# A hybrid decoder step on one core: three adaLN weight loads issued before x, small vectors issued from the ACT queue

## The chip, the cores and the metric

The kernel runs on one core of a Trainium2 chip. The metric is the device time of one execution in microseconds, as the median of several runs; lower is better.

## The reference, cut to what matters

One inference step of a two-layer trunk for a prompt of 256 tokens and eight samples of eight tokens, 2048 features, float32. Each of the four sub-layers (GLA and S5 side by side, a SwiGLU FFN, an mLSTM, a second SwiGLU FFN) is wrapped in the same way:

```python
def modulate(x, c, ada_w, ada_b, norm_g):
    mod = jax.nn.silu(c.astype(jnp.float32)) @ ada_w + ada_b
    shift, scale, gate = jnp.split(mod[:, None, :], 3, axis=-1)
    return rmsnorm(x, norm_g) * (1.0 + scale) + shift, gate

h, gate = modulate(x, c, p["ab_ada_w"][j], p["ab_ada_b"][j], p["ab_norm_g"][j])
z = (h @ p["ab_w_in"][j]).astype(f32)
...
x = x + (gate * out).astype(x.dtype)
```

So the first big product, `h @ ab_w_in`, needs three things first: x and its norm, `c` after silu, and the products of silu(c) with the shift and scale columns of `ab_ada_w` ([2048, 6144]). Outputs are the normed x and all the updated states.

## The kernel before, in words

**Layout.** Activations are kept feature-major, 16 chunks of [128 features, 320 tokens]. Big products stream their weights through TensorE as 128x128 blocks; each block is split by ACT (`hi`) and VectorE (`lo`) into two float32r parts, and three passes (`hi`, `lo` against `xh`, `hi` against `xl`) are summed in PSUM. The adaLN products and the mixing layers run as background tasks between the blocks.

**adaLN steps.** Class `Ada` cuts the four adaLN products into 192 steps. A step (L477) multiplies silu(c) (`cT`) by one tile of weights of 1024 KB, [128, 4, 512]; four steps give 512 columns of `mod`, which `post` (L459) transposes and adds the bias to. `load` (L444) issues the weight loads on SP's queue, one for every free buffer, as far as `limit`. In the startup there are five buffers (two in `ADAM["raw"]`, one in `ex`, two in `ex2`), and a buffer is free again once its step has run. From step 12 (`TEMP`) on the two of `ex2` are given up. Before the load of step 8 (`L6`), `load` issues four loads of `ab_w_in` (`L2`). The startup works in four groups of features: group g needs 8 steps, the shift and the scale of its 512 features, and then `norm_g` (L744) makes its part of the operand.

**Startup, in the order of the program.** SP loads the identity (L312). ACT's queue loads `c_prompt` and `c_sample` (L630, L631). SP loads x in three pieces, 1024, 1024 and 512 KB (L635 to L637), then 13 small vectors (`items`, L619: biases and gains as rows of 128, 2 to 24 KB each) into `rows` (L640 to L645), then the weights of the first five adaLN steps (L652). PE transposes `c`; VectorE halves it, ACT takes its tanh (L659), VectorE makes `cT` (L661, L662). `load_x` (L836) then squares x on ACT with a sum per token (L843), transposes x on TensorE in 16 chunks of three transposes with a VectorE copy each (L844 to L849), transposes `rows` after chunk 7 (`vectors`, L664), and runs one adaLN step after chunk 7 and one after chunk 15 (L852 to L854). A dozen small VectorE instructions and one product then give the norm factors R (L856, L857). The main program (L2345 to L2365) runs the other steps of group 0, its norm, and then the first products; between products it goes on with steps and loads.

**The order of emission.** Each engine and each queue runs its instructions in the order in which the program emits them, and that order is made by an estimate, `Est` (L130). `Est.note` adds an assumed duration for every instruction; a DMA from SP or ACT goes through one assumed generator, 0.45 us each, and one assumed transfer rate of 360 GB/s (L173 to L180). A background task is resumed when, by the estimate, what it waits for is there (`tick`, L383). `spare` (L497) emits an adaLN step only if the estimate says that its weights have landed. So a changed assumption in `Est` can move instructions everywhere in the program, though it costs nothing itself.

`RQ` (L354) chooses the queue of the 13 vectors: 0 is SP, 1 is ACT. ACT's queue belongs to ScalarE: a DMA that waits there holds up the activations behind it.

Of the kernel before, what the change touches and what calls it, by code (L numbers as in the profile page):

```python
"""One step of the conditioned hybrid decoder trunk (GLA + S5, SwiGLU, mLSTM, SwiGLU) on one core.

Activations are kept feature-major: [128 features, 320 tokens] per chunk, tokens 0-255 the prompt,
256 + 8 b + t the samples. Every big product streams its weights through the tensor engine as
stationary 128x128 blocks. A float32 product is carried by three float32r passes: each operand is
split exactly into hi (what float32r keeps) + lo (the rest), and hi.hi + hi.lo + lo.hi is summed in  # L6
PSUM. Mixing layers and the adaLN products run as background tasks between the blocks of the stream.
"""
# [4 lines left out]
F32 = mybir.dt.float32  # L13
# [19 lines left out]
def _consts():  # L33
    """Constants that depend on shapes alone, packed as [128, NC1 + NC2] (float32), and their offsets."""
# [61 lines left out]
class Mem:  # L96
    """Words of a slab of SBUF, handed out first fit."""
# [32 lines left out]
class Est:  # L130
    """What is known beforehand of the instructions' durations (us). Only the order of emission goes by it: a task is
    resumed when what it issued before should be done, so that the engines seldom wait for one another."""

    def __init__(self):
        self.t = dict.fromkeys(("PE", "DVE", "ACT", "POOL", "SP", "DGE", "DMA"), 0.0)
        self.wr, self.rd, self.alias = {}, {}, {}
        self.end = 0.0
# [23 lines left out]
    def note(self, eng, op, a, k):  # L161
# [11 lines left out]
        if op == "dma_start":  # L173
            if eng == "POOL":
                t = self.t[eng] = t + 1.2
            else:
                self.t[eng] = t + 0.06
                t = self.t["DGE"] = max(self.t["DGE"], t) + 0.45
            t = self.t["DMA"] = max(self.t["DMA"], t + 0.65) + 4e-3 * int(np.prod(out.shape)) / 360
# [30 lines left out]
class Eng:  # L210
    """An engine whose instructions are noted in an Est."""
# [14 lines left out]
class Pair:  # L226
    """Up to 256 output columns of one weight matrix; ks: k-chunks in the order they are used."""
# [6 lines left out]
def trunk(tc, a, o, coff, dbg=None, stop=None):  # L234
# [5 lines left out]
    with (  # L240
# [38 lines left out]
        def mps(keep=False):  # L279
            """A bank for results that are read before the task yields; with keep until drop()."""  # L280
# [14 lines left out]
        def kept():  # L295
            """A bank to be kept, as one of two at most."""
            while len(held) > 1:
                yield GO
            return mps(True)
# [4 lines left out]
        # ------------------------------------------------------------------ fixed memory  # L304
# [42 lines left out]
        # ------------------------------------------------------------------ scheduling  # L347
# [6 lines left out]
        NX, TEMP, RQ, VK, SK, L6, L2 = 2, 12, 0, 7, 8, 8, 4  # L354
# [4 lines left out]
        def due(y):  # L359
            """A task yields a number of ticks to wait at least, GO, or what has to be there before it goes on."""  # L360
            t = est.end
            if y is GO:
                return clock[0] + 1, 0.0
            if isinstance(y, int):
                return clock[0] + y, t
            return clock[0] + 1, max(est.ready(x) for x in y)

        def spawn(gen, rank=5):
            """Tasks of a lower rank are looked at first."""
# [19 lines left out]
        def warm():  # L389
            """A product that nobody reads, lest the tensor engine's clock falls."""  # L390
# [3 lines left out]
        def idle(until):  # L394
            """Nothing for the tensor engine in the program before that time."""
# [8 lines left out]
        def go(gen):  # L404
            """A task that the program waits for."""
# [25 lines left out]
        # ------------------------------------------------------------------ adaLN products  # L431
        class Ada:
# [64 lines left out]
            def spare(self):  # L497
                """A step if its weights are there."""
# [12 lines left out]
            def drip(self):  # L511
                """A step every `gap` ticks up to step `last`, as the program sets them."""
# [8 lines left out]
        # ------------------------------------------------------------------ weight stream  # L521
# [3 lines left out]
        def add(*pairs):  # L525
            """Pairs whose units take turns."""
# [24 lines left out]
        def split_to(n):  # L551
            """hi and lo of the first n half units, which are two chunks of k."""
# [46 lines left out]
        # ------------------------------------------------------------------ startup: vectors  # L599
# [18 lines left out]
        # feature vectors as rows of 128, transposed into columns  # L618
# [8 lines left out]
        # c: silu'd, transposed, padded to 32 columns  # L627
# [4 lines left out]
        # x comes in token-major  # L632
        xt_b = M["S"].get(3 * 2048)
        xt = xt_b.v(3, 2048)
        for i in range(2):  # L635
            sp.dma_start(out=xt[:, i, :], in_=a["x_prompt"][0, i * P:(i + 1) * P, :])
        sp.dma_start(out=xt[0:64, 2, :], in_=a["x_sample"].rearrange("b t d -> (b t) d"))  # L637
        pool.memset(rows, 0.0)
# [7 lines left out]
        ada = Ada()  # L646
        ex = [M["G"].get(2048)]
        ex2 = [M["S"].get(2048) for _ in range(NX)]
        keep = list(ada.free)
        ada.free += [b.v(4, 512) for b in ex + ex2]  # L650
        ada.temp = {id(x): x for x in ada.free[3:]}
        ada.load()  # L652
# [30 lines left out]
        # ------------------------------------------------------------------ RMS norm of x and the operand of the next stage  # L683
        def sq_chunk(k, last=False):
            """Adds x chunk k's squares to the sum (the last two go to the tensor engine by themselves)."""
# [13 lines left out]
        def sums(sq):  # L699
            """Column sums of the tiles in sq, token-major ([128, 3], the third column tokens 192-319)."""  # L700
# [9 lines left out]
        def rsqrt_tok(s, n):  # L710
            """(s / n + EPS) ** -0.5"""
# [4 lines left out]
            # a start within 5% by halving the exponent in the bits, then Newton steps  # L716
# [9 lines left out]
        def rsqrt_t(s, n, skip):  # L726
            """The same for the 320 tokens, in PSUM over all partitions."""
# [16 lines left out]
        def norm_g(L, g, R, ht):  # L744
            """Chunks 4 g to 4 g + 3 of XH + XL = rmsnorm(x) * (1 + scale) + shift."""
# [38 lines left out]
        def norm_h(L):  # L784
            """The first half of the next operand; the rest comes between the first products."""
# [9 lines left out]
        def after_norm(pr):  # L795
            """Marks the pair that begins with half an operand."""
# [9 lines left out]
        def resid(L, k, ps, sq):  # L806
            """x chunk k += gate * ps."""
# [13 lines left out]
        def to_out(k):  # L821
            """x chunk k times the last norm's gains, token-major (block 2: tokens 192-319); all but the scale per token."""
# [13 lines left out]
        def load_x():  # L836
            """Feature-major x, and its norm from the token-major one."""
            sm_b, s_b = M["S"].get(8), M["S"].get(2048)
            sm = sm_b.v(3)
            pool.memset(sm_b.v(8), 1.0)  # L840
            for i in range(3):
# [21 lines left out]
        # ------------------------------------------------------------------ S5: per-state constants  # L863
        # partition = (group of the pair, state); a pair holds two groups of 16 channels
# [4 lines left out]
        def s5_setup():  # L869
            bb = S5["bb"] = S5["bb_b"].v(2, 32, 16)  # L870
            # the imaginary parts of a, b and the states are kept negated, so that Re(c h) is a plain sum of products;
            # powers 1 to 4 of a, and for the scan a^4, a^8 and a^16 as (re, re) and (-im, im)
# [39 lines left out]
            def exp(out, x):  # L912
                """exp to float32 accuracy: 2^n by its exponent bits, the rest by a polynomial."""
# [14 lines left out]
            def sine(out, x, quarter):  # L928
                """sin(x + quarter * pi / 2)."""
# [1515 lines left out]
```

## Time and profile before

| what | us |
|---|---|
| median of three runs | 3397.55 |
| lowest and highest run | 3381.38 and 3400.94 |
| span of the profiled execution, first to last instruction | 3383.8 |

The profile gives no time of the profiled execution apart from its span, 3383.8 us, which lies between the lowest and the highest of the timed runs. The chain of waits is read from the last instruction backwards: each piece is what released the next one. The windows give the busy time of each engine in a stretch, the granted TensorE clock (1.00 is 2.4 GHz) and the rate of the 16 DMA engines together. A wait for a DMA in the queue's own waits is time in which the queue issued nothing.

### The profile page before, as it was taken

The page shows a single profiled execution, that of the slowest core. Times are in us where ns is not written, and L with a number is a line of the kernel's source. Part 1 is how long each engine was busy: PE and PEld are TensorE (multiplying, and loading weights), DVE is VectorE, ACT ScalarE, POOL GpSimd, SP SyncE. Part 2 cuts the span into 40 slices and gives each one's busy share as a digit, 9 for nine tenths or more (in the row PEclk, how much of TensorE's full clock was granted, in tenths as well). Part 3 has the DMA queues.
Part 4 walks back from the last instruction along what each step waited for, and adds up shares of the span by engine and source line. Part 5 has one row for each costly group of instructions (what it writes and reads, how often), then busy time and mean ns, then how long its engine had stood idle before and what let it go on. Part 6 is the DMA issues. An engine that isn't in the chain of part 4 may idle for free.

```text
span 3383.8 us, 57931 instructions
## 1 busy us (share of the span) xinstructions
PE 3287.9 (97%) x22802; PEld 3023.7 (89%) x22802; DVE 1870.4 (55%) x3921; ACT 1327.8 (39%) x2509; POOL 336.9 (10%) x508
## 2 busy tenths in 40 slices
PE   7899889999999999999999999999999999999998
PEld 4687778887877799999998899999899999999997
DVE  3768767663344345445465665566645545545546
ACT  2354554343323333433434433344433343343343
POOL 0225511220000000000031000002200000000002
PEclk9999999999999999999999999999999999999999
DMA  9886678779999954444455665556564444444443
GB/s 305 291 264 219 194 259 305 269 240 322 317 318 320 320 171 149 150 152 148 151 170 145 191 194 144 177 187 206 184 207 149 152 150 150 150 150 150 150 150 100
DMA packets 597794, 686.66 MB, mean 203 GB/s; under 512 B 41097, under 2 KB 495057, under 8 KB 596945
## 3 DMA queue, kind: packets, MB, share of 16 engines
q1 hardware_dynamic: 594464, 680.26, 61.7%
q8 instruction: 179, 2.93, 0.3%
q10 hardware_dynamic: 3056, 2.70, 0.2%
q14 instruction: 95, 0.77, 0.1%
HBM read 643.19 MB, written 39.69 MB: 202 GB/s over the span
## 4 chain that ended last, share of the span: by engine, by line
PE 87%; DMA 5%; DVE 4%; ACT 2%; POOL 1%; issue 1%; SPq 0%; ACTq 0%; DVEq 0%; POOLq 0%
PE mm L220 74%; PE misc L220 8%; PE ada L220 5%; DVE S_slab L220 1%; POOL S_slab L220 1%; DVE lo L220 1%; DMA fix_slab<-in_ffn_ada_w_dram 1%; DVE X_slab L220 1%; DVE G_slab L220 1%; DMA R_slab<-in_state_mlstm_C_dram 1%; DMA fix_slab<-in_ab_w_in_dram 0%; DMA fix_slab<-in_ml_ada_w_dram 0%; DMA G_slab<-in_ab_ada_w_dram 0%; DMA fix_slab<-in_ab_ada_w_dram 0%; ACT hi L220 0%
## 5 line engine op out<-in xcount | busy, mean ns | idle before, releaser
L220 DVE TENSOR_TENSOR lo<-fix_slab,hi 128x512 fp32r<-128x512 f32 (+1 forms) x1556 | 1087.1, 704 | 1173.0 <-ACT hi L220 1168.9
L220 ACT CAST hi<-fix_slab 128x512 fp32r<-128x512 f32 (+1 forms) x1556 | 944.3, 612 | 1425.2 <-PE mm L220 1366.6
L220 PE MATMUL mm<-xh,hi 128*128 128x320 f32 x4704 | 1491.6, 317 | 9.7 <-DVE S_slab L220 5.9
L220 PE MATMUL mm<-xl,hi 128*128 128x320 f32 x4704 | 1460.7, 311 | 0.8 <-DVE xl L220 0.6
L220 PE MATMUL mm<-xh,lo 128*128 128x320 f32 x4704 | 1460.1, 310 | 0.9 <-DVE lo L220 0.9
L220 PEld LDWEIGHTS mm<-xh,hi 128*128 128x128 f32 x4704 | 888.4, 189 | 121.8 <-issue 88.0
L220 PEld LDWEIGHTS mm<-xh,lo 128*128 128x128 f32 x4704 | 889.2, 189 | 2.4 <-DVE lo L220 1.8
L220 PEld LDWEIGHTS mm<-xl,hi 128*128 128x128 f32 x4704 | 888.1, 189 | 2.2 <-DVE xl L220 2.2
L220 PE MATMUL mm<-ffh,hi 128*128 128x320 f32 x1408 | 437.8, 311 | 0.0
L220 PE MATMUL mm<-ffh,lo 128*128 128x320 f32 x1408 | 434.3, 308 | 0.0
L220 PE MATMUL mm<-ffl,hi 128*128 128x320 f32 x1408 | 434.3, 308 | 0.0
L220 POOL TENSOR_TENSOR X_slab<-X_slab 128x320 f32<-128x320 f32 (+1 forms) x117 | 109.9, 940 | 2062.4 <-DVE X_slab L220 2016.1
L220 PEld LDWEIGHTS mm<-ffh,hi 128*128 128x128 f32 x1408 | 264.4, 188 | 18.4 <-issue 17.6
L220 PEld LDWEIGHTS mm<-ffh,lo 128*128 128x128 f32 x1408 | 264.5, 188 | 0.0
L220 PEld LDWEIGHTS mm<-ffl,hi 128*128 128x128 f32 x1408 | 264.3, 188 | 0.0
L220 PE MATMUL ada<-fix_slab 128*32 128x512 f32 x1432 | 193.9, 616 | 12.7 <-DMA fix_slab<-in_ab_ada_w_dram 8.7
L220 POOL TENSOR_TENSOR S_slab<-S_slab 128x32 f32<-128x32 f32 (+3 forms) x226 | 119.5, 538 | 78.3 <-ACT S_slab L220 34.1
L220 DVE SCALAR_TENSOR_TENSOR ffs<-ffs,mm 128x320 f32<-128x320 f32 x176 | 81.4, 488 | 29.9 <-ACT ffs L220 23.8
L220 DVE SCALAR_TENSOR_TENSOR X_slab<-mm,fix_slab,X_slab 128x256 f32<-128x256 f32 x176 | 84.6, 480 | 16.7 <-PE mm L220 16.5
L220 PE MATMUL misc<-fix_slab 128*128 128x128 f32 (+1 forms) x454 | 73.1, 287 | 5.7 <-ACT fix_slab L220 5.6
L220 PEld LDWEIGHTS misc<-fix_slab 128*128 128x128 f32 x454 | 59.2, 171 | 18.2 <-ACT fix_slab L220 7.0
L220 PEld LDWEIGHTS ada<-fix_slab 128*32 128x32 f32 x1432 | 29.0, 108 | 51.0 <-issue 34.0
(151 smaller groups left out, 1812.9 us busy)
## 6 DMA issues: line engine op xcount, KB each, us to landing
fix_slab<-in_ffn_w_dram SPq DMA_DIRECT2D x524, 512.0 KB, 3.5
fix_slab<-in_ffn_ada_w_dram SPq DMA_DIRECT2D x96, 1024.0 KB, 7.6
fix_slab<-in_ml_ada_w_dram SPq DMA_DIRECT2D x48, 1024.0 KB, 7.2
fix_slab<-in_ml_w_in_dram SPq DMA_DIRECT2D x96, 512.0 KB, 4.4
fix_slab<-in_ab_ada_w_dram SPq DMA_DIRECT2D x35, 1024.0 KB, 8.0
fix_slab<-in_ab_w_in_dram SPq DMA_DIRECT2D x64, 512.0 KB, 6.5
R_slab<-in_state_mlstm_C_dram SPq DMA_DIRECT2D x32, 512.0 KB, 4.1
out_dram<-R_slab SPq DMA_DIRECT2D x32, 512.0 KB, 6.5
```

Source lines behind the costliest of these rows:

```text
L220: r = call(*a, **k)
```

## The change

Four things are edited. The buffers of the adaLN weights are set up earlier, and the loads of steps 0 to 2 are issued on SP before x, those of steps 3 and 4 right after x. The 13 small vectors are issued from ACT's queue (`RQ` = 1), after `c_prompt` and `c_sample` and, in the program, after the loads of steps 3 and 4; the memset of `rows` comes earlier. `load_x` runs steps 0 to 2 (each followed by `load`) before the squares and the transposes of x; the steps after chunks 7 and 15 are then steps 3 and 4. `Est` assumes a generator of its own for SP and for ACT, and 395 GB/s in place of 360. Comments and docstrings are dropped, which shifts no instruction.

```diff
@@ Est @@
-        self.t = dict.fromkeys(("PE", "DVE", "ACT", "POOL", "SP", "DGE", "DMA"), 0.0)
+        self.t = dict.fromkeys(("PE", "DVE", "ACT", "POOL", "SP", "DGESP", "DGEACT", "DMA"), 0.0)
...
-                t = self.t["DGE"] = max(self.t["DGE"], t) + 0.45
-            t = self.t["DMA"] = max(self.t["DMA"], t + 0.65) + 4e-3 * int(np.prod(out.shape)) / 360
+                t = self.t["DGE" + eng] = max(self.t["DGE" + eng], t) + 0.45
+            t = self.t["DMA"] = max(self.t["DMA"], t + 0.65) + 4e-3 * int(np.prod(out.shape)) / 395
@@ constants @@
-        NX, TEMP, RQ, VK, SK, L6, L2 = 2, 12, 0, 7, 8, 8, 4
+        NX, TEMP, RQ, VK, SK, L6, L2 = 2, 12, 1, 7, 8, 8, 4
@@ startup @@
         xt = xt_b.v(3, 2048)
+        pool.memset(rows, 0.0)
+        ada = Ada()
+        ex = [M["G"].get(2048)]
+        ex2 = [M["S"].get(2048) for _ in range(NX)]
+        keep = list(ada.free)
+        ada.free += [b.v(4, 512) for b in ex + ex2]
+        ada.temp = {id(x): x for x in ada.free[3:]}
+
+        ada.limit = 3
+        ada.load()
         for i in range(2):
             sp.dma_start(out=xt[:, i, :], in_=a["x_prompt"][0, i * P:(i + 1) * P, :])
         sp.dma_start(out=xt[0:64, 2, :], in_=a["x_sample"].rearrange("b t d -> (b t) d"))
-        pool.memset(rows, 0.0)
+        ada.limit = 32
+        ada.load()
         n = 0
         for name, ap, cnt in items:
...
             (sp, act)[RQ].dma_start(out=rows[r:r + cnt, blk, :], in_=ap.rearrange("(k p) -> k p", p=P))
             n += cnt
-        ada = Ada()
-        ex = [M["G"].get(2048)]
-        ex2 = [M["S"].get(2048) for _ in range(NX)]
-        keep = list(ada.free)
-        ada.free += [b.v(4, 512) for b in ex + ex2]
-        ada.temp = {id(x): x for x in ada.free[3:]}
-        ada.load()
@@ load_x @@
             pool.memset(sm_b.v(8), 1.0)
+            for _ in range(3):
+                ada.step()
+                ada.load()
             for i in range(3):
                 r = 64 if i == 2 else P
                 act.activation(s_b.v(2048)[0:r], xt[0:r, i, :], AF.Square, accum_out=sm[0:r, i:i + 1])
```

## Rows read from the trace of the kernel before

**Rows 1.** Busy time by stage: us, engines with instruction counts, PEclk, DMA share, GB/s.

```profile
0.00:220.00 220.00, 183.66 (x1162) 139.08 (x1162) 127.94 (x343) 88.45 (x172) 35.43 (x61) 0.95 0.85 288
220.00:420.00 200.00, 182.80 (x1361) 155.77 (x1361) 149.73 (x376) 95.36 (x230) 102.27 (x210) 0.97 0.67 216
420.00:3384.00 2964.00, 2921.47 (x20283) 2728.85 (x20279) 1592.70 (x3204) 1144.04 (x2107) 199.16 (x238) 0.99 0.60 196
```

**Rows 2.** Chain of waits, 0 to 200 us: start us, us, what.

```profile
11.91 7.59 PE misc L220 x25
19.50 1.87 PE ada L220 x8
21.37 5.06 PE misc L220 x24
26.43 0.99 PE ada L220 x8
...
31.28 7.83 DMA G_slab<-in_ab_ada_w_dram
39.15 1.52 PE ada L220 x8
...
49.23 3.86 PE mm L220 x12
...
67.75 1.04 PE ada L220 x8
68.81 7.65 DMA G_slab<-in_ab_ada_w_dram
```

**Rows 3.** Busy time in four stretches of the start; last two columns DMA share, GB/s.

```profile
2.00:4.00 2.00, 0.25 (x1) 0.18 (x1) 0.00 (x0) 0.92 (x1) 0.00 (x0) 1.00 0.89 240
4.00:8.00 4.00, 0.69 (x2) 0.29 (x2) 0.43 (x3) 0.56 (x2) 0.00 (x0) 1.00 1.00 412
8.00:17.00 9.00, 5.56 (x18) 2.94 (x19) 2.92 (x8) 5.66 (x6) 0.00 (x0) 1.00 0.55 124
17.00:35.00 18.00, 17.30 (x107) 8.41 (x110) 8.90 (x28) 0.58 (x1) 0.00 (x0) 1.00 1.05 402
```

**Rows 4.** Timeline of SP's queue: start us, us, engine line op out<-in xcount.

```profile
1.17 0.90 SPq L220 DMA_DIRECT2D S_slab<-in_x_prompt_dram  x2
...
2.73 0.57 SPq L220 DMA_DIRECT2D S_slab<-in_ab_ada_b_dram  x1
...
6.56 0.31 SPq L220 DMA_DIRECT2D S_slab<-in_ml_ada_b_dram  x1
...
9.38 2.82 SPq L220 DMA_DIRECT2D S_slab<-in_ffn_norm_g_dram  x2
...
13.84 0.29 SPq L220 DMA_DIRECT2D S_slab<-in_gla_b_gate_dram  x1
```

**Rows 5.** Waits of SP's queue, 0 to 14 us: total us, times, longest us.

```profile
SPq L220 <- DMA S_slab<-in_x_sample_dram: 2.2, 1, 2.2
SPq L220 <- DMA S_slab<-in_x_prompt_dram: 2.0, 1, 2.0
SPq L220 <- DMA S_slab<-in_c_sample_dram: 1.8, 1, 1.8
```

**Rows 6.** Timeline of ACT and its queue, first 50 us.

```profile
1.16 0.44 ACTq L220 DMA_DIRECT2D S_slab<-in_c_sample_dram  x1
1.64 1.28 ACT L220 ACT_TABLE_LOAD   x1 [1.64 <-PEq L2433]
7.44 2.12 ACT L220 ACTIVATE S_slab<-S_slab 128x144 f32<-128x144 f32 x2 [4.52 <-DVE S_slab L220]
```

**Rows 7.** Timeline of DVE: the copy of the finished norm factors.

```profile
30.26 0.49 DVE L220 COPY S_slab<-misc 128x320 f32<-128x320 f32 x1 [1.03 <-PE misc L220]
```

**Rows 8.** Busy time in two stretches of the mixing stage; columns as in rows 1.

```profile
300.00:340.00 40.00, 33.98 (x247) 27.85 (x240) 28.31 (x57) 16.74 (x37) 24.15 (x47) 0.96 0.68 220
...
380.00:420.00 40.00, 32.38 (x229) 27.35 (x227) 32.70 (x82) 18.05 (x50) 11.88 (x18) 0.91 0.67 209
```

## The prediction

> **What bounds the kernel now.** I read busy time by stage first. From 420 us on TensorE is busy for 2921 of 2964 us; the first 220 us hold 36 us of its idle time and the next 200 hold 17 [rows 1]. All that the change moves lies in the first 35 us, so only the startup can pay directly, and 1% of the whole is 34 us. Next the chain of waits through the startup: TensorE transposes x from 11.91, steps 0 and 1 of the adaLN products run at 19.50 and 26.43, and then the chain goes over a weight load, 31.28 to 39.1 us, that step 7 waits for; step 7 ends at 40.67, and the first big product starts at 49.23 [rows 2]. Then the stretches: the DMA engines move 412 GB/s from 4 to 8 us, only 124 from 8 to 17, and 402 from 17 to 35 [rows 3]. The timeline of SP's queue says why there is a hole: the 13 vectors are issued from 2.73 to 14.13, and the weights come only after them [rows 4]. At 402 GB/s the hole is (402 - 124) / 402 x 9 = 6.2 us. That is the most by which the weights can come earlier if no byte is moved faster.
>
> The 11.4 us of vector issues are not all issuing. SP waited 1.8 us for `c_sample`, 2.0 for x_prompt, 2.2 for x_sample [rows 5], and `c_sample` was issued by ACT. Counted in order of issue over both queues (c_prompt, identity, c_sample, two x_prompt, x_sample, then the vectors), the waiting vectors are the 11th, 13th and 14th DMA, and what they wait for are the 3rd, 5th and 6th: each waits for the one eight before it. I conclude that the program has eight completion slots, handed out in turn over both queues, and that a ninth DMA waits wherever it stands. The other 5.4 us are 13 issues at some 0.4 us.
>
> **The change part by part.** *Loads ahead of x.* SP's queue holds identity, steps 0 to 2, x, steps 3 and 4: about nine issues at 0.4 us, done by 5 us if nothing waits. The bytes up to x are 3 x 1.05 + 2.62 + 0.33 for vectors, c and identity = 6.1 MB. The stretch from 2 to 4 us moves 0.48 MB [rows 3]; the rest at 402 GB/s ends at 4 + 5.62 / 0.402 = 18.0 us. So x lands 6 us later than the 11.9 of now. Steps 0 to 7 and x together are 11.3 MB and end at 4 + 10.8 / 0.402 = 30.9 us, where the load of step 7 now lands at 39.1 [rows 2] (6.2 us of that is the hole; the rest is weights of the first products that pass in between). For that, the loads of steps 5 to 7 must be issued before the first 8.1 MB run dry at about 23 us, so steps 0 to 2 must be run by then.
>
> *Steps 0 to 2 ahead of the transposes.* They need `cT`. Now VectorE gives ACT its input so that tanh starts at 7.44 [rows 6]; `cT` follows within a microsecond. *Vectors on ACT.* They stand in front of tanh. Without waits 13 x 0.4 = 5.2 us from 1.6 and the table load of 1.28 [rows 6] give a tanh at 8.1, 0.7 us later. With waits it depends on who got the eight slots. If they are handed out in the order of time, few of the vectors have a big load eight places before them: one waits for `c_sample` (6.56, [rows 4]), one or two for the load of step 0 or 1 (about 6 and 8.5 us), and tanh comes at 10 to 11. If in the written order, it is a rival below. No row shows a DMA wait on ACT's queue; I bound the delay of tanh by 0 and 18 us and take 3 us, nearest to the wait on `c_sample`. `cT` is then there at 11, and the three steps take 3 x 1.87, the slow step of row 19.50 [rows 2], to 17. This lies in front of the landing of x, so it costs nothing; cover is gone once tanh comes after about 12. Their buffers come free at 13, 15 and 17, before 23. On SP a slot can hold up x by the same rule; I allow 0.5 us (bounds 0 and 1.5).
>
> *TensorE after x.* Its speed is read from durations: a step takes 1.87 us at 19.50 and 0.99 at 26.43, 25 transposes 7.59 and 24 later ones 5.06 [rows 2]. The granted clock reads 1.00 in both [rows 3], so it doesn't tell the two apart. From 18.5: eight chunks 6.0 (between 5.06 and 7.3), vectors 0.8, step 3 1.0, eight chunks 5.1, `post` 0.8, step 4 1.0: 33.2. The norm factors are done 4.3 us after the last chunk now (26.43 to 30.75, [rows 2, 7]), here at 35.7; steps 5 to 7, 3 x 1.0, fill that time, with their weights landed at 30.9. Step 7 ends at 36.2 in place of 40.67: 4.5 us gained. Bounds: everything early and fast 33.6 (7.1 gained), x at 19.5 with slow chunks and a slow step 3 39.5 (1.2 gained). So TensorE, not DMA, is late next: what stood in the shade of the hole, 16 chunks, now comes after x.
>
> *After step 7* the same chain of 8.6 us leads to the first product. The next stalls begin when a load is issued right after a step gives up its buffer: step to 68.81, load from 68.81 to 76.46 [rows 2]; such a pair moves along as a whole, so the gain is carried on. The DMA lead is 6.2 and TensorE's 4.5, so up to 1.7 us more can come out of a later wait; I take 1.
>
> *`Est`.* No instruction is added, but tasks may be emitted at other places. Bounds: nothing, or the stalls of the mixing stage one and a half times over or gone by half. TensorE idles 6.0 and 7.6 us in its two worst stretches and 17 in all [rows 8, 1]: -9 to +9 us. I take 0, as from 420 us on TensorE is 98.6% busy at any order of the rest.
>
> Sum: -4.5 - 1 = -5.5 us, in the profiled execution 3383.8 to 3378.3. The median of the runs lies 13.8 us above that span, so I put the same step on the median: 3397.55 - 5.5 = 3392.
>
> One rule of the Trainium skill speaks against the part with the queue: "DMA: Bandwidth & Descriptors", in the section "Issuing engines are not separate DMA queues", says that starting DMAs from several engines saves only the time of issuing, which is usually small beside the transfer. Here the trace shows issuing and its waits as 11.4 us for vectors of less than 0.2 MB, so "small" doesn't hold, while the rest of the rule does: nothing moves faster. By the rule alone this part would give nothing, and the sum would stay as it is, because with the weights ahead of x the vectors on SP would be hidden as well.
>
> **The rivals.** *1. ACT's queue becomes the bound (slower).* If slots go in the written order, the vectors follow x and steps 3 and 4: the eighth vector waits for the load of step 4, 8.1 MB, at 4 + 7.6 / 0.402 = 23 us. Five more issues, the table load and tanh put `cT` at 27, steps 0 to 2 end at 33 (3 x 1.87), and only then TensorE starts on x. The sum of above from 33, all at full speed (5.1 + 0.6 + 1.0 + 5.1 + 0.8 + 1.0 + 3.0 = 16.6), ends at 49.6: 9 us later than now, 3406.5. It decides once tanh starts later than about 16, where the 4.5 us are used up. For it: SP's waits are real, and they name DMAs of the other queue. Against: the count of eight fits the order of issue in time; but before the change that is nearly the written order, so the rows can't part the two.
>
> *2. The gain is absorbed.* Later waits on weights (7.7 us at 68.81) end when the DMA engines have done their backlog and not when TensorE comes; then it starts waiting 4.5 us earlier and gets nothing: 3397.5. For it: 402 GB/s from 17 to 35, no slack. Against: the load of that wait is issued only at the end of the step before it.
>
> *3. Another order in the mixing stage,* 9 us either way on top of the forecast: 3383 or 3401. For it: the estimate changes everywhere. Against: the weights are loaded at 196 GB/s on average after 420 us [rows 1], far under both assumed rates.
>
> **How the numbers follow.** Forecast 0.50, own range 3388 to 3396 (1.2 to 7.1 gained, plus 0 to 2); rival 1 0.17; rival 2 0.18; rival 3 0.15. The predicted time is 3392. The runs of the kernel before scatter over 20 us, so a median can be off by some 8 to 15 either way: the range goes from 3368 (3383 - 15) to 3414 (rival 1 and 8). A measurement tells about 1%, 34 us, from no change; no case reaches that, and I leave 0.04 for a reordering that gives more than I bound, and 0.05 for one that costs more: faster 0.04, same 0.91, slower 0.05.
>
> **What would show it.** Right: no stretch under 350 GB/s between 4 and 23 us; steps 0 to 2 on TensorE between 9 and 17; x landing at 18 to 19; step 7 ending at 34 to 39; the first product at 42 to 47. Wrong: ACT's queue waiting for DMAs until after 16 us with a second hole in the rate after 23 (rival 1); a first product at 45 but the same idle time by 220 us as now, at the same place (rival 2); idle time from 220 to 420 us more than 5 us away from 17 (rival 3). The forecast fails altogether if the time moves by more than 34 us.

## The result, and the profile after

| what | before | changed |
|---|---|---|
| median, us | 3390.43 (4 runs) | 3429.22 (4 runs) |
| lowest and highest, us | 3381.38 and 3400.94 | 3422.59 and 3435.09 |
| span of the profiled execution, us | 3383.8 | 3428.4 |

The changed kernel is slower: ratio 1.0116, 95% interval 1.0087 to 1.0144, some 39 us. The device time of a profiled execution is its span and 1.8 us. The profile of before, 3385.6, is thus a fast one of its runs, so differences of traces come out some 5 us larger than those of medians.

The same three stages as [rows 1], windows of the changed kernel:

```profile
0.00:220.00 220.00, 182.08 (x1141) 138.12 (x1141) 126.83 (x334) 87.53 (x167) 34.59 (x61) 0.92 0.87 289
220.00:420.00 200.00, 176.97 (x1209) 152.68 (x1209) 137.55 (x337) 84.72 (x202) 96.32 (x206) 0.89 0.57 184
420.00:3428.00 3008.00, 2951.53 (x20422) 2752.96 (x20422) 1612.99 (x3250) 1156.60 (x2141) 204.43 (x241) 0.99 0.60 195
```

Little changed in the first 220 us. In the next 200 TensorE does 152 matmuls fewer, idles 23.0 us in place of 17.2, and its granted clock reads 0.89 in place of 0.97. After 420 us it does 139 more, in part those that came late, and idles 56.5 us in place of 42.5.

A finer view goes by work and not by time. The 18336 matmuls of the big products run in the same order in every variant, so the k-th of one trace can be held against the k-th of another. Lateness in us against the trace of before, at the start of matmul k, counted from 0 ("old", "new" and other rates are the rate that `Est` assumes):

| k | stage that has just passed | changed | new rate alone | old rate, all else changed |
|---|---|---|---|---|
| 0 | startup | 0.4 | -0.3 | 9.4 |
| 800 | | 4.2 | 1.7 | 7.6 |
| 1200 | first mixing | 20.8 | 18.1 | 11.4 |
| 2400 | first mixing ends | 27.0 | 19.2 | 12.2 |
| 5200 | first FFN | 38.2 | 34.4 | 11.9 |
| 8800 | | 38.2 | 34.4 | 11.9 |
| 10400 | mLSTM | 47.2 | 43.6 | 18.0 |
| 18335 | end | 44.5 | 42.8 | 16.4 |

So the loss has two main places: the mixing stage before k = 2400 and the first FFN. Neither lies in the startup, the part whose instructions were rewritten.

Two cautions on this table. The k-th matmul compares two orders fairly only where the same background work stands before it: at k = 2400 both orders have run 80 adaLN steps and at 8800 both 176, but at 1200 the old order has run 48 steps and 249 instructions of GpSimd, the new one 47 and 281. And it holds single traces against one trace. Two of the kernels below, the one with the hole alone and the one with TensorE kept busy, have, behind the startup, the same order as the kernel before, and its time (ratios 0.9998 and 1.0007). Yet their traces stand 5.5 and 6.8 us late at k = 2400, and 8.9 and 10.4 at 10400. A lateness of that size says nothing.

The startup of the changed kernel, in the stretches of [rows 3]:

```profile
2.00:4.00 2.00, 0.25 (x1) 0.18 (x1) 0.00 (x0) 0.00 (x0) 0.00 (x0) 1.00 0.76 203
4.00:8.00 4.00, 0.48 (x1) 0.18 (x1) 0.31 (x1) 0.00 (x0) 0.00 (x0) 1.00 0.87 268
8.00:17.00 9.00, 3.72 (x20) 1.13 (x24) 0.47 (x2) 2.32 (x3) 0.00 (x0) 1.00 1.05 411
17.00:35.00 18.00, 15.29 (x63) 6.76 (x55) 7.38 (x16) 5.88 (x7) 0.00 (x0) 0.72 1.04 365
```

The hole from 8 to 17 us is filled (411 GB/s for 124), but 4 to 8 us fell from 412 to 268. The chain of waits says why, and it answers to [rows 2]:

```profile
1.17 5.79 DMA fix_slab<-in_ab_ada_w_dram
6.98 3.96 DMA S_slab<-in_ffn_norm_g_dram
10.95 0.34 SPq L220
11.34 0.43 SPq L220
11.81 9.73 DMA S_slab<-in_x_sample_dram
21.59 7.59 PE misc L220 x25
29.18 1.87 PE ada L220 x8
31.05 5.40 PE misc L220 x28
...
42.14 1.43 PE misc L220 x10
...
49.67 3.86 PE mm L220 x12
```

SP's queue stood still three times ahead of x, 8.6 us in all (its waits from 0 to 14 us):

```profile
SPq L220 <- DMA S_slab<-in_c_sample_dram: 4.1, 1, 4.1
SPq L220 <- DMA S_slab<-in_ffn_norm_g_dram: 2.6, 1, 2.6
SPq L220 <- DMA S_slab<-in_ffn_ada_b_dram: 1.9, 1, 1.9
```

The load of step 1 waited for `c_sample`, that of step 2 for the sixth vector, and x for the seventh. ACT's queue could issue that one only at 6.98, 2.5 us after the sixth, when the load of step 0, 5.79 us under way, had landed. So x is issued only at 10.95 and lands at 21.59. The semaphore that each DMA names in the trace shows the eight slots of the prediction at work, in turn over both queues. But the turn is neither the written order nor that of who is ready first: SP was ready for the load of step 1 at 1.6 us, yet that load has the eleventh turn, behind six vectors that ACT went on issuing until 4.52. In the end the first product starts at 49.67, where it was 49.23.

### The profile page after: what moved, and what is told of

It is laid out like the page before. It is cut to its first block, busy times and chain, and to the rows that moved or that the text cites. A ratio compares the mean times of both kernels' runs of the same rounds, so it can differ in the third digit from the quotient of the medians.

```text
span 3428.4 us, 57878 instructions
## 1 busy us (share of the span) xinstructions
PE 3310.6 (97%) x22772; PEld 3043.8 (89%) x22772; DVE 1877.4 (55%) x3921; ACT 1328.8 (39%) x2509; POOL 335.3 (10%) x508
## 4 chain that ended last, share of the span: by engine, by line
PE 83%; DMA 9%; DVE 4%; ACT 2%; POOL 1%; issue 1%; SPq 0%; ACTq 0%; DVEq 0%; POOLq 0%
PE mm L220 70%; PE misc L220 8%; PE ada L220 5%; DMA fix_slab<-in_ml_ada_w_dram 2%; DMA fix_slab<-in_ffn_ada_w_dram 2%; DVE S_slab L220 1%; DMA R_slab<-in_state_mlstm_C_dram 1%; DVE lo L220 1%; DMA fix_slab<-in_ab_ada_w_dram 1%; POOL S_slab L220 1%; DVE X_slab L220 1%; DMA UD<-S_slab 1%; ACT S_slab L220 1%; ACT hi L220 0%; DMA G_slab<-in_ab_ada_w_dram 0%
## 5 line engine op out<-in xcount | busy, mean ns | idle before, releaser
L220 DVE SCALAR_TENSOR_TENSOR ffs<-ffs,mm 128x320 f32<-128x320 f32 x176 | 81.6, 488 | 22.6 <-ACT ffs L220 20.3
L220 DVE SCALAR_TENSOR_TENSOR X_slab<-mm,fix_slab,X_slab 128x256 f32<-128x256 f32 x176 | 84.6, 480 | 11.9 <-PE mm L220 11.9
L220 DVE TENSOR_TENSOR S_slab<-S_slab 128x256 f32<-128x256 f32 (+3 forms) x167 | 75.8, 465 | 5.0 <-POOL S_slab L220 1.0
```

The lines of the kernel that those rows point to most:

```text
L220: r = call(*a, **k)
```

## The experiments

Ratios are to the kernel before on the same chip, with 95% intervals. They are not quite the quotient of two medians: for the new estimate alone, below, the medians (3426.21 and 3393.59) give 1.0096 and 32.6 us, the ratio 1.0114 and 39 us.

**The new estimate alone.** The kernel before, with both edits in `Est`:

```diff
-                t = self.t["DGE"] = max(self.t["DGE"], t) + 0.45
+                t = self.t["DGE" + eng] = max(self.t["DGE" + eng], t) + 0.45
-            t = self.t["DMA"] = max(self.t["DMA"], t + 0.65) + 4e-3 * int(np.prod(out.shape)) / 360
+            t = self.t["DMA"] = max(self.t["DMA"], t + 0.65) + 4e-3 * int(np.prod(out.shape)) / 395
```

> The kernel before with nothing but the new estimate (395 GB/s, two generators); the startup is as before. Theory A: 32 to 44 us slower than before, with the loss between the stream's products 500 and 2100 and again after 8880. Theory B: within 6 us of before.

Measured: 3426.21 us, ratio 1.0114 (1.0092 to 1.0137). An assumption that adds no instruction carries the whole loss. It is the rate: with the second generator alone the emitted program is the one of before, instruction by instruction, and with the rate alone it is this one. The startup edits leave the order after the startup as it is, too. With 395 step 168 of the adaLN products stands before matmul 4704 of the big products, with 360 before 4857.

**All else, with the old estimate.** The changed kernel with the generator and the rate of before.

```diff
-                t = self.t["DGE" + eng] = max(self.t["DGE" + eng], t) + 0.45
-            t = self.t["DMA"] = max(self.t["DMA"], t + 0.65) + 4e-3 * int(np.prod(out.shape)) / 395
+                t = self.t["DGE"] = max(self.t["DGE"], t) + 0.45
+            t = self.t["DMA"] = max(self.t["DMA"], t + 0.65) + 4e-3 * int(np.prod(out.shape)) / 360
```

> The change with the estimate as before (one generator, 360 GB/s). Theory A, the assumed rate reorders the program after the startup: within 6 us of the kernel before, first big product at 49 to 50 us. Theory B, the startup itself (slots, ACT's queue) costs the time: 30 us or more slower than before, like the change.

Measured: 3399.4 us, ratio 1.0026 (1.0008 to 1.0044). The startup edits cost some 6 us (medians) to 9 us (ratio) where a gain of 5.5 was forecast. In the profiled run x landed at 25.77, TensorE's granted clock was at its lower level all through what follows, and the first product came at 58.6:

```profile
20.00:26.00 6.00, 0.71 (x2) 0.36 (x2) 0.00 (x0) 3.55 (x5) 0.00 (x0) 0.51 0.99 300
26.00:32.00 6.00, 6.00 (x21) 3.08 (x20) 3.31 (x7) 1.81 (x2) 0.00 (x0) 0.50 1.05 404
32.00:40.00 8.00, 8.00 (x31) 3.49 (x29) 3.50 (x9) 0.58 (x1) 0.00 (x0) 0.50 1.06 376
```

The changed kernel issues the same in its startup and reached it at 49.67: x landed 4.2 us earlier there, and the granted clock, at 0.50 from about 20 us on in both traces, rose at 31.5 us and not at 47.4. So one startup varies by some 9 us between two traces, and the medians are the better witness.

**The queue alone,** in the kernel before.

```diff
-        NX, TEMP, RQ, VK, SK, L6, L2 = 2, 12, 0, 7, 8, 8, 4
+        NX, TEMP, RQ, VK, SK, L6, L2 = 2, 12, 1, 7, 8, 8, 4
```

> The kernel before with the 13 vectors on ACT's queue and nothing else. Theory A with the slots as I read them: the weights are issued some 8 us earlier, the first product comes 2 to 6 us earlier, the whole is 0 to 6 us faster. Theory B: ACT's queue alone costs, 5 us or more slower.

Measured: 3393.66 us, ratio 1.0002 (0.9982 to 1.0021): nothing. The vectors' own time on SP was hidden, or moved: x landed at 15.3 in place of 11.9, because its second issue waited 5.2 us for a slot (that of `c_sample`). The rule of the Trainium skill that the prediction set aside ("DMA: Bandwidth & Descriptors", section "Issuing engines are not separate DMA queues": only issue time is saved, and that is usually small) gave the right answer for this part.

**The loads and steps without the queue:** the kernel of the old estimate above, with `RQ` at 0 again.

```diff
-        NX, TEMP, RQ, VK, SK, L6, L2 = 2, 12, 1, 7, 8, 8, 4
+        NX, TEMP, RQ, VK, SK, L6, L2 = 2, 12, 0, 7, 8, 8, 4
```

> The change with the estimate as before and the vectors on SP's queue: only the loads ahead of x and steps 0 to 2 ahead of the transposes. Theory A with the slots as I read them: tanh as early as before (7.5 us), x landing near 18 us, first product 3 to 6 us earlier than before, the whole 0 to 6 us faster. Theory B: the order of loads costs, 5 us or more slower.

Measured: 3398.9 us, ratio 1.0024 (1.0008 to 1.0040). x landed at 19.4, but the vectors, now behind the weights, were issued until 27.1 and held TensorE after the first eight chunks until 28.4. First product at 54.3.

**The loads ahead of x, steps where they were,** on the kernel before.

```diff
+        ada.limit = 3
+        ada.load()
         for i in range(2):
             sp.dma_start(out=xt[:, i, :], in_=a["x_prompt"][0, i * P:(i + 1) * P, :])
         sp.dma_start(out=xt[0:64, 2, :], in_=a["x_sample"].rearrange("b t d -> (b t) d"))
+        ada.limit = 32
+        ada.load()
```

> The kernel before with the loads of steps 0 to 2 issued before x and those of steps 3 and 4 right after it, but steps 0 to 2 left where they were (after chunks 7 and 15 of x and after the second half), vectors on SP's queue behind, old estimate. It separates the order of the loads from the order of the steps. By the theory that x is only delayed by the bytes put in front of it: x lands at 18 to 19.5, TensorE has nothing to do before, its transposes run at the slow level (7.4 to 7.7 for 25), and the first product comes at 55 to 58, 6 to 9 us later than before, 2 to 6 us later than with the steps moved as well (54.3); at the end 8 to 15 us are left. Rival (only the early steps cost, by starting TensorE slow): first product at 50 to 52 and less than 4 us at the end.

Measured: 3400.39 us, ratio 1.0036 (1.0021 to 1.0052); x at 19.77, first product at 59.1. The order of the loads costs by itself; the medians don't part this kernel from the one with the steps moved as well. A second stall joins, which the sum on the delay of x alone did not hold: SP's queue waits for a slot behind the big loads, then issues the vectors, and TensorE waits for the last of them:

```profile
5.98 19.14 DMA S_slab<-in_ab_ada_w_dram
25.14 0.31 SPq L220
...
27.08 1.36 DMA S_slab<-in_gla_b_gate_dram
28.44 0.14 issue
28.58 0.45 PE misc L220
```

**The hole alone:** the kernel before with the loop that issues the vectors on SP moved behind the five weight loads, and `vectors` after chunk 15.

```diff
-        NX, TEMP, RQ, VK, SK, L6, L2 = 2, 12, 0, 7, 8, 8, 4
+        NX, TEMP, RQ, VK, SK, L6, L2 = 2, 12, 0, 15, 8, 8, 4
...
         ada.load()
+        n = 0
+        for name, ap, cnt in items:
...
```

> The kernel before with the vectors issued on SP after the first five weight loads, and transposed after chunk 15: x stays first, ACT's queue is free, the estimate is as before. If the hole in the DMA rate was worth what I predicted: no hole, the load of step 7 landing near 31 us, TensorE next, the first product 3 to 6 us earlier and the whole 3 to 6 us faster. If TensorE's slow start bounds: first product within 2 us of before.

Measured: 3392.82 us, ratio 0.9998 (0.9983 to 1.0013). The rate from 8 to 17 us rose to 333 GB/s, that from 17 to 35 fell to 261, and the first product came at 50.5:

```profile
8.00:17.00 9.00, 4.94 (x16) 2.51 (x16) 2.85 (x7) 5.93 (x7) 0.00 (x0) 1.00 1.03 333
17.00:35.00 18.00, 17.87 (x70) 7.93 (x70) 8.11 (x26) 0.00 (x0) 0.00 (x0) 1.00 0.76 261
33.29 0.37 SPq L220 DMA_DIRECT2D G_slab<-in_ab_ada_w_dram  x1
```

So by itself the hole of [rows 3] was worth nothing: TensorE bounded the startup. The third line, from SP's timeline, is the load of step 7, which needs the buffer of step 2. SP issued it when that step had run, at 33.29 here and at 31.28 before [rows 2], and step 2 stands behind the transposes of x. With steps 0 to 2 ahead of x, as the prediction had it, this run doesn't try the hole.

**TensorE kept busy before x:** the kernel before with 14 products that nobody reads after the transposes of `c` (each stands as two instructions in the trace, x28).

```diff
         act.activation(th, ct, AF.Tanh)
+        wps = mps()
+        for _ in range(14):
+            pe._raw.matmul(wps[:, 0:P], ones, ident, start=True, stop=True)
```

> The kernel before with 14 products that nobody reads, put on TensorE right after the transposes of c, where it otherwise stands idle from 7.3 to about 9.4 and again to 11.9 us; they are not noted in the estimate, so that the order of everything else stays. Theory S (TensorE's slow level in the startup bounds the time from x to the first product, and it is the idle time ahead of it that lets it fall): the 25 transposes after x take 5.0 to 5.5 us in place of 7.6, step 0 takes 1.0 in place of 1.9, and the first product comes 3 to 4 us earlier, 45 to 46. Rival (the slow level comes of something else, or the weight load of step 7 bounds): the transposes stay at 7.4 to 7.7, or they get fast and step 7 waits for its weights so much longer; the first product within 1 us of 49.2 to 50.7. In the median 0 to 4 us less than before, which lies within the scatter of the runs.

Measured: 3392.76 us, ratio 1.0007 (0.9992 to 1.0023); first product at 50.3. The timeline of TensorE:

```profile
6.94 5.97 PE L662 MATMUL misc<-fix_slab 128*128 128x128 f32 x28
12.74 5.06 PE L220 MATMUL misc<-fix_slab,S_slab 128*128 128x128 f32 x27
19.95 1.94 PE L220 MATMUL ada<-fix_slab 128*32 128x512 f32 x8 [2.14 <-DMA fix_slab<-in_ab_ada_w_dram]
21.82 7.38 PE L220 MATMUL misc<-fix_slab,S_slab 128*128 128x128 f32 x24
```

The first eight chunks take 5.06 us in place of 7.59, as theory S has it, but they end before step 0's weights are there. TensorE waits 2.1 us, and the other eight chunks then run at the lower clock (granted 0.50 from 20 to 32 us), 7.38 in place of 5.06. It loses later what it gained early.

**The rate by stages.** 395 until the end of the GLU that closes the mixing stage and 360 after it, and the other way round.

```diff
+        self.rate = 395
...
-            t = self.t["DMA"] = max(self.t["DMA"], t + 0.65) + 4e-3 * int(np.prod(out.shape)) / 360
+            t = self.t["DMA"] = max(self.t["DMA"], t + 0.65) + 4e-3 * int(np.prod(out.shape)) / self.rate
...
+            est.rate = 360
```

> The kernel before with 395 GB/s assumed from the start to the end of the mixing stage (to the first products with ab_w_out) and 360 from there on. Theory A1, the two losses are apart and add: 15 to 23 us slower than before, all of it before the stream's product 2400, the FFN's steps as far apart as before. Theory A2, the loss comes from the steps in the FFN alone: within 5 us.

> The other half: 360 GB/s until the end of the mixing stage, 395 from there on. Theory A1: 18 to 28 us slower than before, 15 of it between the products 2400 and 5200 as waits of TensorE for adaLN weights, the rest after 8880. Theory A2: 30 us or more.

Measured: 395 in the mixing stage alone 3413.29 us, ratio 1.0067 (1.0043 to 1.0091): 22.8 us late at k = 2400, 22.5 at 8800. 395 after it alone 3406.16 us, ratio 1.0043 (1.0024 to 1.0062): 4.2 us early at 2400, 10.0 late at 5200. The two losses are separate and add up: 0.67% and 0.43%, for 1.14% with both.

The FFN's loss is plain in TensorE's waits from 700 to 1215 us. Before:

```profile
PE ada L220 <- DMA fix_slab<-in_ffn_ada_w_dram: 0.8, 1, 0.8
PE ada L220 <- DMA fix_slab<-in_ml_ada_w_dram: 0.5, 2, 0.3
```

With the new rate only after the mixing stage:

```profile
PE ada L221 <- DMA fix_slab<-in_ml_ada_w_dram: 7.2, 13, 1.2
PE ada L221 <- DMA fix_slab<-in_ffn_ada_w_dram: 6.5, 10, 1.6
```

13.7 us of waits, and 14.2 us lost from k = 2400 to 5200. Such a wait comes from steps that stand ahead of their weights. Next, what the DMA engines moved in this stretch. Before, 720 to 1190 us:

```profile
q1 hardware_dynamic: 101856, 149.38, 91.5%
```

and with the new rate alone, 740 to 1200 us:

```profile
q1 hardware_dynamic: 97872, 145.10, 90.1%
```

That is 319 and 316 GB/s (all queues), at a share of 90% or more. From step 88 to 168 the old order has 25.7 matmuls of the big products to a step, the new one 23.9. With 3.71 us for 24 matmuls, 1.0 for a step and 0.44 for the four transposes after every fourth step, a period is 5.08 or 4.80 us at full speed (5.07 were measured before). A step brings 1.049 MB, a matmul a third of a block of 64 KB, 0.022 MB: 1.61 MB in 5.08 us is 317 GB/s, 1.57 in 4.80 is 327. So the old order asks for what is moved and the new one for some 3% more. I estimate the loss at 80 steps x (1.57 / 0.316 - 4.80), some 13 us if 316 was all there was; 11 to 15 were measured in the three kernels with 395 here.

That the DMA engines could give no more is not shown. SP's queue itself stood still for most of these 460 us, with the new rate alone:

```profile
SPq L220 <- DVE lo L220: 274.5, 75, 5.9
SPq L220 <- DVE fix_slab L220: 89.7, 18, 6.5
```

The first line is the wait for VectorE's `lo`, after which the buffer of a block of the big products is free again (before, 288.4 us from 740 to 1200). A step's load that stands behind such a block's load on SP is issued late whatever the DMA engines can do, and no run here tells the two apart.

**Other rates.** The kernel before with 340, 350 and 375; the first of them:

```diff
-            t = self.t["DMA"] = max(self.t["DMA"], t + 0.65) + 4e-3 * int(np.prod(out.shape)) / 360
+            t = self.t["DMA"] = max(self.t["DMA"], t + 0.65) + 4e-3 * int(np.prod(out.shape)) / 340
```

> The kernel before with 340 GB/s assumed. If too early steps are the FFN's loss, then no loss there (TensorE's waits for adaLN weights at most 2 us between the products 2400 and 5200) with steps some 29 products apart. In the mixing stage: if a faster estimate as such is the harm, this is the same as before or up to 10 us faster; if any other order costs, 5 to 20 us slower.

> The kernel before with an assumed rate of 350 GB/s. FFN steps come later in the program than at 360 (step 168 before product 5013 in place of 4857), so by theory A the FFN loses nothing and TensorE waits for adaLN weights there less than 3 us; the mixing stage has yet another order and by theory A (the order at 360 is an especially good one) loses 10 to 25 us by product 2000: 3404 to 3419. Theory B (distance from the old rate): about 60 percent of what 340 cost, 7 to 8 us by product 2000, 3402. Theory C (chance): anything from -10 to +5 us by product 2000.

> The kernel before with an assumed transfer rate of 375 GB/s in place of 360, nothing else; the generator of DMAs is as before. The FFN steps then come nearly as early in the program as at 395 (step 168 before stream product 4707, where 360 has 4857 and 395 has 4704); the order in the mixing stage is a third one. Theory A (two losses: steps ahead of their weights in the FFN, and an order of the mixing stage that fits less well): the FFN loses about 14 us between products 2400 and 5200, paid as waits of TensorE for ffn_ada_w and ml_ada_w, and the mixing stage loses 10 to 30 us by product 2000; in all 3410 to 3430 where before is about 3394. Theory B (the loss grows with the distance from the old rate): about 44 percent of the 33 to 39 us, so 15 us in all, 3409, in both stages alike. Theory C (the mixing loss at 395 and 340 was chance, most orders cost nothing): only the FFN's 14 us, 3408, with no more than 5 us lost at product 2000.

| assumed GB/s | ratio (95%) | late at 2400, us | 2400 to 8800, us | 8800 to the end, us |
|---|---|---|---|---|
| 340 | 1.0048 (1.0031 to 1.0065) | 23.8 | -0.6 | 0.8 |
| 350 | 1.0025 (1.0007 to 1.0042) | 9.7 | 0.1 | 9.5 |
| 360 | 1 | 0 | 0 | 0 |
| 375 | 1.0030 (1.0014 to 1.0046) | 0.4 | 11.3 | -0.5 |
| 395 | 1.0114 (1.0092 to 1.0137) | 19.2 | 15.2 | 8.4 |

The FFN's loss goes with the rate: none up to 360, 11.3 and 15.2 us above. The mixing stage's doesn't: 375 loses nothing there, 340 and 395 a good 20 us. The 9.7 of 350 is hardly more than the 5.5 and 6.8 us that two traces with the order of before show there. That is neither "any other order is worse" nor "the farther off the worse"; it has to do with which order comes out.

**What the mixing stage loses.** Matmuls 800 to 1200 hold most of it, 16.4 us, though not all of that is loss, since the new order has more of the background work in this stretch. First before, then the new rate alone, windows from the one to the other:

```profile
261.80:365.10 103.30, 95.20 (x695) 80.66 (x694) 81.01 (x196) 48.36 (x111) 63.56 (x139) 0.98 0.68 223
```

```profile
263.50:383.20 119.70, 109.44 (x749) 93.22 (x748) 85.27 (x203) 52.34 (x120) 70.41 (x165) 0.90 0.57 184
```

TensorE is not idle much longer (10.3 us for 8.1). It does more, 749 instructions for 695, and it is slower. The granted clock of 0.90 over 119.7 us is 12.0 us of full clock lost, for 2.1 before. Over all matmuls up to 2400 this sum is some 17 us before and 38 with the new rate, and each fall from 1.00 to 0.50 stands behind a pause of TensorE. So the clock is a suspect. To try it I filled the pauses with products that nobody reads, in both orders, as many ahead of an instruction that waits as a table in the kernel says:

```diff
         def noted(*a, **k):
+            if self._name == "PE":
+                fill(self, a[0])
             r = call(*a, **k)
```

> The kernel before with the new estimate alone (the other order of emission, +33 to +39 us), with 109 unread products ahead of 14 instructions of TensorE that wait in both traces of that order, all before product 2400. Theory H (most of the loss in the mixing stage is TensorE at half its clock after pauses that the other order leaves): the sum of (1 - granted clock) x time from product 0 to 2400 falls from 38 to under 22, and the time by 12 to 20 us, to a ratio of 1.004 to 1.008 over before, of which some 14 us are the waits of the FFN for its weights. Rival O (the pauses themselves and VectorE's and ACT's own work are the loss; the clock only follows): the granted clock rises with the unread products, but product 2400 comes at the same time within 4 us as without them; ratio 1.010 to 1.012.

> The kernel before, same order and same estimate, with 84 products that nobody reads put on TensorE ahead of 11 of its instructions that wait 0.8 us or more in every trace of that order (for ACT, VectorE, GpSimd or a DMA): as many as fill some 85 percent of the wait at full clock. Theory H (in the mixing stages part of the time goes because TensorE's granted clock falls to half after such a pause, and the pauses let it fall): the sum of (1 - granted clock) x time from product 400 to 2400 falls from the 11 of the kernel before to under 4, in layer 1 from 11.6 to under 6, and the time falls by 6 to 14 us. Rival (the pause itself is all that is lost, or the clock falls for another cause): the granted clock falls as before and the time stays within 3 us or grows by the products that don't fit, up to 5 us.

Measured: with the new rate 3442.91 us, ratio 1.0153 (1.0137 to 1.0169), worse still; with the old 3393.48, ratio 1.0004 (0.9991 to 1.0017). Matmuls 800 to 1200, to within 1.5 us, with the new rate and filled pauses:

```profile
263.10:384.90 121.80, 108.37 (x800) 92.21 (x800) 87.28 (x206) 52.82 (x120) 71.02 (x167) 0.96 0.57 182
```

The granted clock rose from 0.90 to 0.96, and the stretch took 121.8 us in place of 119.7. A faster TensorE only waited more (13.4 us idle for 10.3). In this stretch the clock follows and doesn't set the time. In others the trial was poor: in about half of the places the unread products, which write the bank of the instruction behind them, themselves waited, came after the pause and pushed the work back (5.7 us of them at 399.5, 5.8 at 419.7). There it says nothing on the clock, and from 1200 to 1600 the granted clock even fell lower. Over all matmuls up to 2400 the clock lost fell only from some 38 to 32 us, where theory H wanted under 22, so for the rest of the mixing stage the clock is not ruled out.

What may set the time is read from the chain of waits. Before:

```profile
272.52 0.82 POOL S_slab L220
...
286.17 0.59 POOL S_slab L220
...
293.04 3.56 POOL S_slab L220 x4
```

From 270 to 302 us it is GpSimd alone, one small instruction after another, and TensorE and VectorE run their stream products and splits beside it. With the new rate:

```profile
269.82 7.85 DMA fix_slab<-in_ab_ada_w_dram
...
288.90 0.43 DVE S_slab L220
...
291.70 1.29 DVE lo L220 x2
...
301.29 0.92 DVE S_slab L220
...
303.77 1.12 DVE lo L220
...
340.25 2.36 POOL S_slab L220 x3
```

The chain goes over the load of a step and then, from 285 to 306, over VectorE, which does the mixing's small work and the `lo` splits of the stream in turn. GpSimd's chain comes from 338 on. The tasks meet on VectorE where before one of them ran on GpSimd beside it. I read this from the two chains; no run shows it, since no kernel took the splits or the small work away from VectorE in that order.

## Why the prediction was wrong

**The step that failed** is the term for `Est`: "I take 0, as from 420 us on TensorE is 98.6% busy at any order of the rest", with bounds of -9 to +9 us. It measured +33 (medians) to +43 us (traces): the new rate alone, with no instruction added, puts the tasks in another order, and that order costs some 20 us in the mixing stage and some 15 in the first FFN. Three things in it were wrong. TensorE's 98.6% was taken as a property of the kernel, and it was one of the order at 360. The bounds counted only TensorE's idle time, and in the stretch that lost most TensorE was idle hardly longer (10.3 us for 8.1): it was busy longer, with 54 instructions more and at a lower granted clock, while the chain of waits went over other engines. Why that order is worse there stays open, as said above. And "196 GB/s on average after 420 us [rows 1], far under both assumed rates" is an average over stages: in the first FFN the DMA engines move 319 GB/s at 91.5%, and there an order that asks for 327 waits. One window on that stage, from the profile of before, would have shown how little is spare there.

**Rival 3** had the right mechanism, another order that costs, with its mark (idle time from 220 to 420 us more than 5 us away from 17: 23.0), and a size about four times too small. The 0.05 for slower by more than 1% is where the result fell.

**The startup term** of -5.5 failed too: the edits without the new estimate cost some 6 to 9 us. *The hole* is filled, and in the changed kernel step 7 no longer waits for its weights. Nothing came of it, because TensorE comes later: step 7 ended at 42.1, where it was 40.67. That TensorE and not DMA is late next was foreseen; how late was not. *x* was forecast to land at 18.0 to 18.5 and did at 21.59: the slots were weighed for ACT's queue and allowed 0.5 us on SP's, but SP waited 8.6 us there. *tanh* came at 12.28 (10 to 11 forecast) and steps 0 to 2 ran from 13.28 to 18.3 (to 17): about right, and before x. *TensorE after x* was taken at 6.0 us for eight chunks and 1.0 for step 3, and took 7.59 and 1.87. With x 3.1 us late these make 3.1 + 1.6 + 0.9 = 5.6 us, nearly all by which step 7 ended later (42.1 for 36.2). One bound doesn't follow from its sum: 33.6 for "everything early and fast" would need x at 17.0, since the 16.6 us of rival 1 come after it, and the text has 18.0 at the earliest. Rival 1 (ACT's queue until 27) didn't come, since tanh came at 12.28: the slots went in neither of the two orders that the prediction weighed, and in the one that came out the vectors stand ahead of x. Rival 2's way, that later waits take up what the startup changes, is seen with the queue alone, in one trace: 4.7 us late at the first product and none by k = 4000. The old-rate kernel was 9.4 us late there and in its one trace still 11.9 at k = 4000.

## What to carry to other kernels

An estimate that orders a program is a part of the kernel like any other: give a change to it a term of its own, as wide as the whole stage whose order it sets, and measure it alone. Read the transfer rate by stages and not as an average, and ask of each stage whether the new order asks for more bytes per us than are moved there now. And before filling a hole in the transfers, see what waits behind it: if TensorE is late anyway, earlier weights buy nothing.

## What the runs showed of the hardware

A granted clock of 1.00 in the startup need not be a reading. In every trace here the first record of the clock is a rise to 1.00 (at 22.6 us before, at 42.2 with the loads first, at 12.6 with the unread products), and the windows count the time ahead of the first record as 1.00. The durations show that TensorE was slow there. With the loads first the clock reads 1.00 from 20 to 26 us, without a record, and with the unread products 0.50, recorded, at the same speed of transposes (24 in 7.38 us, where 24 take 4.9 to 5.1 at full speed). The 1.00 of [rows 3] ahead of 22.6 us, by which the prediction found the clock of no use, is of the same kind:

```profile
20.00:26.00 6.00, 6.00 (x21) 3.11 (x20) 3.30 (x7) 1.81 (x2) 0.00 (x0) 1.00 0.81 291
```

```profile
20.00:26.00 6.00, 6.00 (x22) 2.32 (x22) 1.90 (x4) 0.00 (x0) 0.00 (x0) 0.50 1.05 403
```

In the startup the 16 DMA engines moved up to 412 GB/s (415 with the hole alone, 4 to 8 us). In the FFN, where two tiles' loads of 512 and 1024 KB take turns, it was 319 at a share of 91.5% in the queue; why less was not tried. A wait for a completion slot passes from queue to queue: x on SP waited for a vector on ACT, which had waited for a weight load on SP.
